# A two-layer hybrid DiT on one core: ada rows loaded two ahead and folded a call later, the gate in four pieces, five attention fetches moved, and the first chunk's columns moved

## The chip, the cores and the metric

The kernel runs on one core of one Trainium2 chip. The metric is the device time of one execution in microseconds (us). A core has TensorE (PE; its weight loads are shown as PEld), VectorE (DVE), ScalarE (ACT), GpSimd (POOL) and SyncE (SP). SP issues most of the loads from DRAM, ScalarE and GpSimd some. Matmuls write to PSUM, which has eight banks of 128 x 512 numbers of 32 bits; the other data are in SBUF.

## The reference

The model has two layers on 256 latent tokens and 256 context tokens, 1024 wide. In short:

```python
for i in range(DEPTH):                       # 2 layers
    mod   = silu_c  @ ada_w[i] + ada_b[i]    # 1024 -> 6 * 1024, for the latent tokens
    mod_c = silu_cc @ ada_w[i] + ada_b[i]    # the same for the context
    sh1, sc1, g1, sh2, sc2, g2 = split(mod)
    h, hc = x * (1 + sc1) + sh1, ctx * (1 + sc1c) + sh1c
    y, yc = retention_mixer(...) if i == 0 else neighbourhood_mixer(...)
    x = layer_norm(ALPHA * x + g1 * y)
    h = x * (1 + sc2) + sh2
    x = layer_norm(ALPHA * x + g2 * (relu(h @ w1[i]) ** 2 @ w2[i]))
    # in layer 0 the same for ctx
```

All matrices are float32. `ada_w` has 2 x 1024 x 6144 numbers, 50 MB, though it is used with two vectors only. The neighbourhood mixer has 32 heads of 32 columns; each latent token attends to a window of latent tokens, with a bias for each place, and to all context tokens.

## The kernel before

**Matmuls in three parts.** TensorE gets each float32 matrix as a high part (`hi`, a rounded copy) and a low part (`lo`, what the rounding left). `mm3` issues three matmuls for each product: high by high, high by low, low by high. A weight unit is 512 KB. `fetch` loads it into a buffer `raw` (SP), ScalarE casts it to `hi`, and VectorE subtracts to get `lo`, which frees `raw`. The pool of `raw` has four buffers, and `hi` and `lo` have five each (`WB`). `take` hands out the next unit and fetches ahead until five are in hand, so a further cast waits until TensorE has used up a unit.

**The ada rows.** `ada_w` is too large for TensorE to be the right place for all of it. `bg_stream` is a generator that works it off in the background, one step for each call of `bg`. A step is one row block of 512 KB (`rawa`, lines 416 to 428 and 482 to 489), in the same four `raw` buffers; VectorE multiplies it by a column of the condition and adds it up (`weigh`, tile `acc`, or `strips` in the early parts), once for each of two vectors. At each step the generator first issues the load of the next row (`nxt`, lines 517 to 522) and then weighs the present one. Eight steps make a part. Then `folded` sums the 32 lanes (`red`) and appends to `due` a function that does the rest: `ada_columns` (four small matmuls per vector into the bank `pada`, and an add into `mods`) or `ada_gate` (a matmul into `pada`, a transpose, an add, and a write of the row to DRAM as `grow`). `bg` calls `flush` first, so what one call appended runs at the start of the next (lines 501 to 503 and 561 to 566). `fold` flushes too. Until the first 31 calls are done the early parts run (`EARLY`); the others run in the MLP of layer 0.

**The MLP of layer 0** (lines 1270 to 1425) has two passes `hf` over the 4096 hidden columns. A pass computes eight pairs of hidden blocks (`p1`, with ReLU and square into `hid`) and then two output halves (`half`); each half has eight units `u` of 24 matmuls into four banks, one for each of four groups of 128 tokens, and one `bg` call after each unit. After a half, `accumulate` multiplies each bank by the gate `G2` on VectorE (`acc<-p,G`) and GpSimd adds the result to `R`. The gate's rows come back from DRAM, spread over the 128 partitions, by `load_gate` at `u == 3` of the first half (line 1359): two loads of 512 KB, issued by ScalarE.

**The attention** of layer 1 (lines 1802 to 1838) is a list of steps by hand. Step n has, in this order: `gather(n + 1)`, `turned(n)`, `early` fetches with their `lo`; `scores(n + 2)` (12 matmuls into four banks `pqk`); `soften(n + 2)` (VectorE adds the bias and takes the least, ScalarE takes the exponential with its sum); `late` fetches with their `lo`; a projection (K, Q or V); `flip(n + 1)` (13 transposes into four banks, copied out as `pt` by ScalarE and VectorE by turns); `invert`; `last` fetches; and `attend(n)`. `STEPS` gives `(early, late, last, projection, after)`.

**The first chunk** (lines 887 to 911). The first layer's modulation is computed in eight chunks of 128 columns, on TensorE. Of chunk 0 the sums are computed (`chunk_sums`), copied (`chunk_row`), the four token groups transposed (`chunk_turn`), and the sums turned into columns (`chunk_columns`, then `mod` on VectorE); with these, `chunk_modulate` writes `hTh`, which the matmuls need. `turn_over` issues matmuls that nothing reads.

**What sets the order.** A scheduler orders the instructions of each engine by the order of the program and by the times at which it expects data and buffers; where an engine's `on` is set, the order of the program is kept. On the chip each engine works in the order it was given. In the first chunks SP, TensorE, ScalarE and VectorE are in program order; in the MLP's loops and the attention steps mostly the scheduler's order holds. A helper records all calls, so most rows of the profile name line 84, and tiles tell them apart.

Of the kernel before, what the change touches and what calls it, by code (L numbers as in the profile page):

```python
# [104 lines left out]
def kernel(  # L105
# [50 lines left out]
    def bank(s="ps"):  # L156
        return psp.tile([P, 512], F32, tag="ps", name=nm(s))
# [279 lines left out]
    def ada_columns(l, w, red, c0, nt):  # L437

        pr = bank("pada")
        for j in range(4):  # L440
            pe.matmul(
                pr[32 * j : 32 * j + 32, 0 : 8 * nt],
                lhsT=cv("fold"),
                rhs=red[:, :nt].rearrange("p t (k j) -> p j (t k)", j=4)[:, j],
                start=True,
                stop=True,
                tile_position=(0, 32 * j),
            )
        dve.tensor_add(
            out=mods[l, w][:, :, c0 : c0 + 4, :],  # L450
            in0=(
                pr[:, 0:16].rearrange("p (t s k) -> p s k t", t=2, s=2)
                if nt == 2
                else pr[:, 0:8].rearrange("p (s k) -> p s k", s=2).unsqueeze(3).broadcast_to([P, 2, 4, 2])
            ),
            in1=acol[:, COLUMNS.index((l, w)), :, c0 : c0 + 4].unsqueeze(3).broadcast_to([P, 2, 4, 2]),
        )
# [24 lines left out]
    def bg_load(l, w, part, offs, n):  # L482

        if (l, w, part) not in EARLY:
            return ada_load(l, n, offs)
        raw = rawp.tile([P, 2, 512], F32, tag="raw", name=nm("rawa"))
        w_ap = ada_w[l][256 * (n % 4) : 256 * (n % 4) + 256, offs[n // 4] : offs[n // 4] + 512]
        sp.dma_start(out=raw[:], in_=w_ap.rearrange("(k p) n -> p k n", p=P))
        return raw
# [8 lines left out]

    due = []

    def flush():
        while due:
            due.pop(0)()

    def bg_stream():


        plan = []
        for l, w, part in (
            list(EARLY)  # L510
            + [(0, 1, 2), (1, 0, 0), (1, 0, 1), (1, 0, 2), (1, 1, 0), (1, 1, 1), (1, 1, 2)]
        ):
            sh, sc, g = 3 * w * D, (3 * w + 1) * D, (3 * w + 2) * D
            offs = (sh + 512 * part, sc + 512 * part) if part < 2 else (g, g + 512)
            for n in range(KC):
                plan.append((l, w, part, offs, n))
        nxt = bg_load(*plan[0])
        yield
        for step, (l, w, part, offs, n) in enumerate(plan):
            raw = nxt  # L520
            if step + 1 < len(plan):
                nxt = bg_load(*plan[step + 1])

            nt = 2 if l == 0 or (w == 0 and part < 2) else 1
            if n == 0:
                red = smp.tile([P, 2, 32], F32, tag="red", name=nm("red"), bufs=2)
            if (l, w, part) in EARLY:
                dve.on = True
                for kk in range(2):
                    for t in range(nt):  # L530
                        weigh(spare(t), raw[:, kk, :], t, 2 * (n % 4) + kk, n % 4 == 0 and kk == 0)
                dve.on = False
                if n % 4 == 3:
                    yield
                    for t in range(nt):
                        folded(red, spare(t), t, 512 * (n // 4), 512)
            else:
                if n == 0:
                    acc = slot(S_VL, [P, 2, D], F32, "acc")
                for t in range(nt):  # L540

                    dve.on = n == 0 and l == 0
                    weigh(acc[:, t], raw[:].rearrange("p a n -> p (a n)"), t, n, n == 0)
                    dve.on = False
                if n == KC - 1:
                    for t in range(nt):
                        folded(red, acc[:, t], t, 0, D)
            if n == KC - 1:
                if part < 2:
                    due.append(lambda a=(l, w, red, 4 * part, nt): ada_columns(*a))  # L550
                else:
                    due.append(lambda a=(l, w, red, nt): ada_gate(*a))
            yield

    bgs = bg_stream()
# [5 lines left out]
    def bg(n=1):  # L561
        for _ in range(n):
            if bg_done[0] < bg_max[0]:
                flush()
                bg_done[0] += 1
                next(bgs, None)

# [273 lines left out]

    KINDS = slice(0, NLAT), slice(NLAT, NT)

    def chunk_turn(k):

        pts[k] = bank("pt")[:, 0:256], prs[k][:, 256:512]
        for t in range(4):
            pe.transpose(pts[k][t // 2][:, tsl(t % 2)], R[t][:, tsl(k)], ident)

    def modulated(e, out_ap, pt, k, a):  # L850
# [47 lines left out]
    turn_over(3)  # L898
    chunk_sums(0, 1)
    chunk_row(0, tsl(1))  # L900
    chunk_turn(0)
    chunk_columns(0)
    turn_over(4)
    w = ws[0]
    w.high(w.Q)
    chunk_modulate(0, lambda: (w.high(w.V), w.low(w.Q)))
# [335 lines left out]


    HS = [S_T0, S_T1, S_SH, S_SL, S_TH, S_TL, S_GS, S_VH]
    LAT, ALL, CTX = slice(0, NLAT), slice(0, NT), slice(NLAT, NT)

    def mm1(us, sl, pb, ks=range(KC), at=0):
# [22 lines left out]
    for hf in range(2):  # L1270
# [67 lines left out]
        for half in range(2):  # L1338
            last = hf == 1 and half == 1
            pb = [bank("p2") for _ in range(4)]  # L1340

            def mm2(t, u, un):
                wh, wl = un
                for kk in range(2):
                    k = 2 * u + kk
                    ht = hid[u]
                    mm3(
                        pb[t][:], (ht[:, kk, 0, tsl(t)], ht[:, kk, 1, tsl(t)]), (wh[:, kk, :], wl[:, kk, :]),
                        k == 0, k == 15,
                    )  # L1350

            nheld = 4 if last else 0
            for u in range(8 - nheld):
                (un,) = take(1)
                for t in range(4):
                    mm2(t, u, un)
                bg()
                if G2 is None and u == 3:
                    G2 = load_gate(0, 1)
            if not last:  # L1360
                for t in range(4):
                    accumulate(pb[t], t, half, G2)
                continue
            bg_until(87)
            held = take(4)
            gb = slot(S_VL, [P, 2, D], F32, "gb")
            ln_tiles(gb, 0, 1)
            xns = []
            for i in range(2):
                xn2 = slot(HS[i], [P, 2, D], F32, "xn")  # L1370
                xns += [xn2[:, 0, :], xn2[:, 1, :]]

            def affine(t, pts):

                return [mod_aff(pts[half], half, t, A, B, halves=t < 2) for half in range(2)]

            def turn(t):
                return [mod_pt(xns[t], half) for half in range(2)]

            def settle(t):  # L1380

                add_to(t, 1, gated(pb[t], t, 1, G2), dve)
                stat(t, 1)
                return moments(t)

            def whiten(t, m):
                shift = shift_of(*m)
                center(t, 0, *m, xns[t], shift)
                center(t, 1, *m, xns[t])

            for t in range(4):
                stat(t, 0)
            ORDER = (pe, act, dve)
            for e in ORDER:
                e.on = True
            for i in range(4):
                mm2(0, 4 + i, held[i])
            A, B = fold(0, 1, 1, 0)
            m = settle(0)
            mm2(1, 4, held[0])  # L1400
            mm2(1, 5, held[1])
            whiten(0, m)
            mm2(1, 6, held[2])
            mm2(1, 7, held[3])
            m = settle(1)
            mm2(2, 4, held[0])
            p = turn(0)
            mm2(2, 5, held[1])
            f = affine(0, p)
            whiten(1, m)  # L1410
            for half in range(2):
                mod_split(f[half], half, 0, pool, True)
            mm2(2, 6, held[2])
            mm2(2, 7, held[3])
            m = settle(2)
            mm2(3, 4, held[0])
            p = turn(1)
            f = affine(1, p)
            for half in range(2):
                mod_split(f[half], half, 1, dve, True)  # L1420
            mm2(3, 5, held[1])
            take(0, 2)
            whiten(2, m)
            mm2(3, 6, held[2])
            mm2(3, 7, held[3])
# [358 lines left out]
    def K(g):  # L1784
        return lambda: k_part(g)

    def Q(p):
        return lambda: q_pair(p)
# [4 lines left out]
    def W(half, t):  # L1793
# [7 lines left out]
    REST = lambda: rest_evac(rest_mm(1))  # L1801
    STEPS = [
        (1, 0, 0, [K(2)], []),
        (2, 0, 0, [K(3)], []),
        (2, 0, 0, [K(4)], []),
        (1, 0, 0, [K(5)], []),
        (2, 0, 0, [Q(2)], []),
        (1, 1, 0, [V(0)], []),
        (0, 0, 0, [V(1)], []),
        (0, 0, 0, [V(2)], [REST]),  # L1810
        (0, 0, 0, [V(3)], []),
# [399 lines left out]
```

## Time and profile before

| | |
|---|---|
| median of 3 runs | 1186.33 us (1186.08 to 1186.82) |
| profiled execution | 1185.37 us, span 1183.3 us |
| granted TensorE clock, mean | 0.997 |
| PE, PEld busy | 1170.2 us, 988.2 us |
| DVE, ACT, POOL busy | 841.4, 480.0, 212.6 us |
| DMA | 195.10 MB, 165 GB/s over the span |

Times in the views are us from the span's start. A timeline's row has start, duration, engine, operation, tiles (what is written, an arrow, what is read), shape and count, and in brackets how long the engine was idle before it and what ended that. A row of the windows has the stretch, its length, the busy time (and the instructions) of PE, PEld, DVE, ACT and POOL, the granted clock as a share of full speed, the DMA engines' busy share and GB/s. A row of the waits has the engine and tile that waited, for whom, the total, how often, and the longest. A row of the chain has start, length and what it was; a DMA's length runs from its issue to its landing. A row of the DMA issues has how many, their size, and the median time from issue to landing. A busy TensorE is not one at its peak, as matmuls overlap, and one that waits inside a matmul is counted as busy.

The MLP of layer 0 runs from about 436 to 796 us, its first output half from about 527 to 570. The attention steps run from about 848 to 970.

### The profile page before, as it was taken

The page shows a single profiled execution, that of the slowest core. Times are in us where ns is not written, and L with a number is a line of the kernel's source. Part 1 is how long each engine was busy: PE and PEld are TensorE (multiplying, and loading weights), DVE is VectorE, ACT ScalarE, POOL GpSimd, SP SyncE. Part 2 cuts the span into 40 slices and gives each one's busy share as a digit, 9 for nine tenths or more (in the row PEclk, how much of TensorE's full clock was granted, in tenths as well). Part 3 has the DMA queues.
Part 4 walks back from the last instruction along what each step waited for, and adds up shares of the span by engine and source line. Part 5 has one row for each costly group of instructions (what it writes and reads, how often), then busy time and mean ns, then how long its engine had stood idle before and what let it go on. Part 6 is the DMA issues. An engine that isn't in the chain of part 4 may idle for free.

```text
span 1183.3 us, 17724 instructions
## 1 busy us (share of the span) xinstructions
PE 1170.2 (99%) x6822; PEld 988.2 (84%) x6822; DVE 841.4 (71%) x1331; ACT 480.0 (41%) x819; POOL 212.6 (18%) x364
## 2 busy tenths in 40 slices
PE   9999999999999999999899999999999999999997
PEld 7788888888888889888788888889878878999886
DVE  3877684876798586897867775668566689877446
ACT  3643332232323255442122333137466666756341
POOL 0102001100200340870203000223344430000001
PEclk9999999999999999999999999999999999999999
DMA  9932551543364226776566665646244334666660
GB/s 277 273 125 92 157 165 48 179 143 107 124 194 146 89 67 222 211 186 227 174 196 202 212 213 189 199 138 203 84 140 125 107 116 160 217 208 200 231 211 37
DMA packets 139091, 195.10 MB, mean 165 GB/s; under 512 B 9936, under 2 KB 81136, under 8 KB 139008
## 3 DMA queue, kind: packets, MB, share of 16 engines
q1 hardware_dynamic: 130880, 182.03, 48.5%
q0 software_dynamic: 6976, 9.39, 3.5%
q10 hardware_dynamic: 1152, 2.56, 0.6%
q8 instruction: 53, 0.87, 0.3%
q14 instruction: 30, 0.25, 0.1%
HBM read 189.12 MB, written 5.75 MB: 165 GB/s over the span
## 4 chain that ended last, share of the span: by engine, by line
PE 85%; DVE 5%; DMA 5%; issue 2%; ACT 2%; POOL 0%; SPq 0%; DVEq 0%; ACTq 0%; POOLq 0%
PE p L84 34%; PE pq L84 8%; PE pv L84 7%; PE pw L84 7%; PE pg L84 7%; PE pn L84 5%; PE pnv L84 4%; PE po L84 3%; DMA rawa<-in_ada_w_dram 2%; DVE acc L84 2%; DMA raw<-in_mlp_w_dram 2%; PE pnw L84 1%; PE pS L84 1%; DVE lo L84 1%; PE ppt L84 1%
## 5 line engine op out<-in xcount | busy, mean ns | idle before, releaser
L84 ACT CAST hi<-raw 128x1024 fp32r<-128x1024 f32 (+2 forms) x228 | 232.1, 1034 | 318.7 <-DMA raw<-in_mlp_w_dram 82.9
L84 DVE TENSOR_TENSOR lo<-raw,hi 128x1024 fp32r<-128x1024 f32 (+2 forms) x228 | 275.0, 1220 | 99.2 <-ACT hi L84 99.1
L84 PE MATMUL p<-hi,hid 128*128 128x512 f32 (+1 forms) x832 | 243.2, 375 | 0.0
L84 PEld LDWEIGHTS p<-hi,hid 128*128 128x128 f32 x832 | 153.0, 189 | 28.2
L84 PE MATMUL p<-hTh,lo 128*128 128x256 f32 (+1 forms) x512 | 165.8, 326 | 0.0
L84 PE MATMUL p<-hTl,hi 128*128 128x256 f32 (+1 forms) x512 | 165.8, 326 | 0.0
L84 PE MATMUL p<-hTh,hi 128*128 128x256 f32 (+1 forms) x512 | 162.9, 328 | 0.0
L84 PE MATMUL p<-lo,hid 128*128 128x512 f32 (+1 forms) x416 | 156.0, 375 | 0.0
L84 DVE SCALAR_TENSOR_TENSOR acc<-rawa,scol,acc 128x1024 f32<-128x1024 f32 x70 | 91.9, 1322 | 66.5 <-DMA rawa<-in_ada_w_dram 66.5
L84 PEld LDWEIGHTS p<-hTh,lo 128*128 128x128 f32 x512 | 96.4, 188 | 8.8
L84 PEld LDWEIGHTS p<-hTl,hi 128*128 128x128 f32 x512 | 96.4, 188 | 8.6
L84 PEld LDWEIGHTS p<-hTh,hi 128*128 128x128 f32 x512 | 94.2, 188 | 8.7
L84 PEld LDWEIGHTS p<-lo,hid 128*128 128x128 f32 x416 | 78.7, 189 | 13.7
L84 ACT CAST hid<-r 128x256 fp32r<-128x256 f32 (+1 forms) x64 | 32.0, 502 | 115.3 <-DVE r L84 115.1
L84 POOL TENSOR_TENSOR rstd<-rstd,misc 128x1 f32<-128x1 f32 x28 | 19.2, 687 | 214.1 <-DVE rstd L84 212.9
L84 DVE SCALAR_TENSOR_TENSOR strips<-rawa,scol,strips 128x512 f32<-128x512 f32 x84 | 57.6, 747 | 0.0
L84 ACT ACTIVATE s<-s,mn 128x512 f32<-128x512 f32 x64 | 45.5, 714 | 26.2 <-DVE mn L84 26.2
L84 POOL TENSOR_SCALAR rstd<-mv 128x1 f32<-128x1 f32 x16 | 3.9, 244 | 290.0 <-DVE mv L84 290.0
L84 POOL TENSOR_TENSOR R<-R,acc 128x512 f32<-128x512 f32 x16 | 24.8, 1566 | 165.9 <-DVE acc L84 165.8
L84 PE MATMUL pw<-hi,oh 128*128 128x512 f32 x128 | 50.9, 398 | 0.0
L84 PE MATMUL pg<-hi,hTh 128*128 128x512 f32 x128 | 50.6, 395 | 0.0
L84 PE MATMUL pw<-hi,ol 128*128 128x512 f32 x128 | 49.9, 390 | 0.0
(236 smaller groups left out, 2328.2 us busy)
## 6 DMA issues: line engine op xcount, KB each, us to landing
raw<-in_mlp_w_dram SPq DMA_DIRECT2D x128, 512.0 KB, 4.5
rawa<-in_ada_w_dram SPq DMA_DIRECT2D x80, 512.0 KB, 3.9
raw<-in_ret_w_in_dram SPq DMA_DIRECT2D x42, 512.0 KB, 3.6
raw<-in_nat_w_in_dram SPq DMA_DIRECT2D x24, 512.0 KB, 4.5
rawq<-in_ada_w_dram SPq DMA_DIRECT2D x16, 512.0 KB, 6.1
raw<-in_ret_w_o_dram SPq DMA_DIRECT2D x16, 512.0 KB, 3.6
bias<-rpb_rows POOLq DMA_DIRECT2D x32, 128.0 KB, 2.9
raw<-in_nat_w_o_dram SPq DMA_DIRECT2D x8, 512.0 KB, 3.7
```

The lines of the kernel that those rows point to most:

```text
L84: r = f(*args, **kwargs)
```

## The change

Four edits are made together.

- `bg_stream` keeps a list of loaded rows. From the first part behind `EARLY` on it loads until two rows beyond the present one are on their way, where it was one.
- Each entry of `due` carries the number of the call that made it. In the MLP `bg` runs only entries that are at least two calls old, so a part is folded into `pada` one call later. In the early parts, and in `fold`, nothing changes.
- The gate of the MLP is loaded in four pieces of 256 KB: at `u == 3` and `u == 4` the first 512 columns of the second and the first row, at `u == 6` and `u == 7` the others.
- In five rows of `STEPS` fetches move: in four of them one or two from `early` to `late`, and a fifth row's one from `early` to the row before as `last`. In chunk 0, two of the four transposes move behind the columns, the pair that did share the bank of the sums gets a bank of its own, and `turn_over` has one matmul fewer.

```diff
-    def flush():
-        while due:
-            due.pop(0)()
+    def flush(before=1 << 30):
+        while due and due[0][0] < before:
+            due.pop(0)[1]()
...
-        nxt = bg_load(*plan[0])
+        loaded = [bg_load(*plan[0])]
         yield
         for step, (l, w, part, offs, n) in enumerate(plan):
-            raw = nxt
-            if step + 1 < len(plan):
-                nxt = bg_load(*plan[step + 1])
+            raw = loaded.pop(0)
+            ahead = 1 if step < len(EARLY) * KC else 2
+            while len(loaded) < min(ahead, len(plan) - 1 - step):
+                loaded.append(bg_load(*plan[step + 1 + len(loaded)]))
...
-                    due.append(lambda a=(l, w, red, 4 * part, nt): ada_columns(*a))
+                    due.append((bg_done[0], lambda a=(l, w, red, 4 * part, nt): ada_columns(*a)))
                 else:
-                    due.append(lambda a=(l, w, red, nt): ada_gate(*a))
+                    due.append((bg_done[0], lambda a=(l, w, red, nt): ada_gate(*a)))
...
             if bg_done[0] < bg_max[0]:
-                flush()
+                flush(bg_done[0] + (bg_max[0] == 31))
...
-    def chunk_turn(k):
-
-        pts[k] = bank("pt")[:, 0:256], prs[k][:, 256:512]
-        for t in range(4):
+    def chunk_turn(k, ts=range(4)):
+
+        if k not in pts:
+            pts[k] = bank("pt")[:, 0:256], (prs[k][:, 256:512] if k else bank("pt")[:, 0:256])
+        for t in ts:
...
-    chunk_turn(0)
+    chunk_turn(0, (0, 1))
     chunk_columns(0)
-    turn_over(4)
+    chunk_turn(0, (2, 3))
+    turn_over(3)
...
-                if G2 is None and u == 3:
-                    G2 = load_gate(0, 1)
+                if hf == 0 and half == 0 and u > 2:
+                    if G2 is None:
+                        G2 = cpool.tile([P, 2, D], F32, tag="G", name=nm("G"))
+                    if u != 5:
+                        t, sl = u % 2 if u < 5 else u - 6, HALF[u > 5]
+                        act.dma_start(out=G2[:, t, sl], in_=grow[0, 1][t : t + 1, sl].broadcast_to([P, 512]))
...
-        (2, 0, 0, [K(3)], []),
-        (2, 0, 0, [K(4)], []),
-        (1, 0, 0, [K(5)], []),
-        (2, 0, 0, [Q(2)], []),
-        (1, 1, 0, [V(0)], []),
+        (0, 2, 0, [K(3)], []),
+        (0, 2, 0, [K(4)], []),
+        (0, 1, 0, [K(5)], []),
+        (0, 2, 1, [Q(2)], []),
+        (0, 1, 0, [V(0)], []),
```

More of the change, by code (lines that the diff above doesn't have):

```diff
@@ L1244 @@
     HS = [S_T0, S_T1, S_SH, S_SL, S_TH, S_TL, S_GS, S_VH]
+    HALF = slice(0, 512), slice(512, 1024)
     LAT, ALL, CTX = slice(0, NLAT), slice(0, NT), slice(NLAT, NT)
```

## The prediction

> **What bounds the kernel now.** I read the page first (busy shares, the chain), then the waits of TensorE alone, then the stretch of the longest of them.
>
> ```profile
> PE 1170.2 (99%) x6822; PEld 988.2 (84%) x6822; DVE 841.4 (71%) x1331; ACT 480.0 (41%) x819; POOL 212.6 (18%) x364
> ```
> ```profile
> PE pada L84 <- DVE acc L84: 3.2, 1, 3.2
> ```
>
> TensorE has work in 99% of the span, so an edit that removes no matmul can win only TensorE's waits. By far the longest that the trace names is `pada`'s, 3.2 us at once, in the MLP. The stretches around it, with the granted clock in the column before the DMA share:
>
> ```profile
> 575.70:578.70 3.00, 0.00 (x0) 0.00 (x0) 2.95 (x4) 1.05 (x1) 0.00 (x0) 1.00 0.14 55
> 578.80:583.20 4.40, 4.38 (x19) 3.47 (x20) 4.40 (x5) 0.00 (x0) 4.35 (x3) 0.61 0.57 165
> 630.00:662.80 32.80, 32.80 (x152) 26.96 (x144) 23.61 (x26) 11.29 (x16) 6.30 (x6) 1.00 0.65 203
> ```
>
> TensorE does nothing for 3 us, and the 4.40 us behind have a granted clock of 0.61 where other stretches have 1.00: another 4.40 x 0.39 = 1.7 us. The place costs 3.2 + 1.7 = 4.9 us.
>
> What makes `pada` late stands in VectorE's timeline and in the chain of waits (a DMA's piece there runs from issue to landing):
>
> ```profile
> 569.91 1.19 DVE L84 TENSOR_TENSOR lo<-raw,hi 128x1024 fp32r<-128x1024 f32 x1
> 571.01 1.41 DVE L84 TENSOR_SCALAR acc<-rawa,scol 128x1024 f32<-128x1024 f32 x2
> 575.75 1.28 DVE L84 SCALAR_TENSOR_TENSOR acc<-rawa,scol,acc 128x1024 f32<-128x1024 f32 x1 [3.33 <-DMA rawa<-in_ada_w_dram]
> 576.95 1.22 DVE L84 TENSOR_TENSOR lo<-raw,hi 128x1024 fp32r<-128x1024 f32 x1
> 578.08 1.28 DVE L84 TENSOR_TENSOR acc<-p,G 128x512 f32<-128x512 f32 x2
> ```
> ```profile
> 540.96 8.89 DMA rawa<-in_ada_w_dram
> ...
> 571.12 4.53 DMA rawa<-in_ada_w_dram
> ```
>
> `pada` does not wait for its own input: `red` was folded before the rows shown. It waits for a PSUM bank. At the start of the second output half all eight banks belong to the two halves, and one comes free with `acc<-p,G`, the gating of the first half. That stands on VectorE behind an ada row issued at 571.12, when VectorE was already beginning the row before it, and landed 4.53 us later. An in-order VectorE waited 3.33 us for it, and TensorE for VectorE.
>
> **The change part by part, the MLP.** Three edits meet here; none adds or takes away a matmul.
>
> Ada rows two ahead: a row is issued one step earlier. The rows and the weights share four raw buffers, and the rows now hold three.
>
> ```profile
> raw<-in_mlp_w_dram SPq DMA_DIRECT2D x15, 512.0 KB, 4.7
> rawa<-in_ada_w_dram SPq DMA_DIRECT2D x13, 512.0 KB, 4.0
> G<-grow ACTq DMA_DIRECT2D x2, 512.0 KB, 7.0
> ```
>
> These are the issues from 520 to 600: 13 rows in 80 us, 6.2 us a row, though TensorE asks for one per weight unit. A unit is 24 matmuls; two units of 24 with the same 512 columns take 5.5 us each by the stretch at 630 (144 weight loads in 32.8 us, 0.228 us each). A row goes: 4.0 us to land, then two `acc` of 1.28 us and a `lo` of 1.22 us between them. Issued a step earlier, the landing lies beside the previous row's 3.8 us of VectorE work; the 3.33 us wait should fall to near nothing, and `acc<-p,G` then ends about 3 us sooner, at some 575.5, just when TensorE comes to `pada`.
>
> Folding one call later: `pada` stands one weight unit later in TensorE's order, so at 575.7 + 5.5 = 581.2. Even with nothing else gained, `acc<-p,G` (first one done by 578.8) is 2.4 us early. Either edit alone takes most of the wait; together they leave about 5 us. I take all of 3.2, and with no idle time before it the slow clock goes too: 4.9 us. Ends: 0, if an equal wait comes up behind it, and 4.9.
>
> [...]
>
> The gate in four pieces: two loads of 512 KB became four of 256 KB at units 3, 4, 6 and 7. ScalarE issues them and waits there for `grow`:
>
> ```profile
> 541.88 1.06 ACT L84 CAST hi<-raw 128x1024 fp32r<-128x1024 f32 x1 [6.13 <-DMA grow<-gate]
> ```
> ```profile
> 566.72 1.06 ACT L84 CAST hi<-raw 128x1024 fp32r<-128x1024 f32 x1 [5.49 <-DMA raw<-in_mlp_w_dram]
> 572.69 1.06 ACT L84 CAST hi<-raw 128x1024 fp32r<-128x1024 f32 x1 [4.91 <-DMA raw<-in_mlp_w_dram]
> 577.21 1.05 ACT L84 CAST hi<-raw 128x1024 fp32r<-128x1024 f32 x1 [3.46 <-DMA raw<-in_mlp_w_dram]
> 586.40 1.06 ACT L84 CAST hi<-raw 128x1024 fp32r<-128x1024 f32 x1 [8.15 <-PE p L84]
> ```
>
> Because the gate's fold also moves a call back, `grow` is complete 5.5 us later, near 547, and a `hi` cast behind the first piece can be held as long. Two more issues lie in idle ScalarE time (6.13 us before this cast). The held cast costs nothing while prepared weights are in hand. How many are: the cast of 586.40 waits for the buffer of the second unit of the second half, five back, so it is the seventh, and the cast of 566.72 the fourth. That unit's `lo`, two casts behind, is the one done by 578.2; TensorE began the half at 575.7 - 5.5 = 570.2 and would come to its fourth unit at 570.2 + 3 x 5.5 = 586.7. The lead is 8.5 us, more than the 5.5. If that cover is gone, 5.5 us come back. The first two pieces are needed when the half ends at 570; 547 plus 7.0 is well ahead. Spread over four units, they also no longer meet the row of 540.96, which took 8.89 us against a median of 4.0. I count 0 for the pieces.
>
> **The attention fetches.** Per step TensorE has one score block, one projection, one flip and one attend. Windows from score block to score block:
>
> ```profile
> 848.20:857.30 9.10, 9.10 (x77) 7.38 (x76) 5.54 (x13) 6.00 (x14) 3.18 (x8) 1.00 0.30 91
> 866.40:875.70 9.30, 9.30 (x83) 7.56 (x76) 6.83 (x17) 5.53 (x14) 4.07 (x10) 1.00 0.51 156
> 875.70:886.00 10.30, 9.98 (x80) 7.73 (x76) 6.75 (x17) 6.46 (x17) 4.50 (x12) 1.00 0.42 120
> 886.00:895.70 9.70, 9.70 (x104) 8.85 (x101) 6.97 (x18) 5.92 (x15) 4.12 (x11) 1.00 0.49 150
> 895.70:905.50 9.80, 9.80 (x80) 7.92 (x76) 6.40 (x18) 6.40 (x16) 4.43 (x11) 1.00 0.42 125
> 905.50:915.30 9.80, 9.80 (x84) 7.73 (x76) 6.93 (x19) 5.91 (x16) 4.30 (x11) 1.00 0.36 107
> 924.90:934.00 9.10, 9.10 (x80) 7.37 (x76) 5.61 (x21) 5.89 (x17) 3.38 (x9) 1.00 0.19 46
> ```
>
> The first and the last row are undisturbed steps (a K and a V projection): 9.1 us. The five between exceed it by 0.2, 1.2, 0.6, 0.7 and 0.7 us: 3.4 us, the most that this edit can win. (The page calls TensorE busy there too: a matmul that waits is counted.) How it comes about, from ScalarE's, VectorE's and TensorE's timelines of the second of these rows:
>
> ```profile
> 872.73 0.73 ACT L84 ACTIVATE s<-s,mn 128x512 f32<-128x512 f32 x1 [2.08 <-DVE mn L84]
> ...
> 876.03 0.85 ACT L84 COPY pt<-ppt 128x384 f32<-128x384 f32 x2
> ```
> ```profile
> 868.61 0.29 DVE L84 TENSOR_TENSOR oTl<-rt,oTh 128x128 fp32r<-128x128 f32 x1 [0.37 <-ACT oTh L84]
> 869.72 2.36 DVE L84 TENSOR_TENSOR lo<-raw,hi 128x1024 fp32r<-128x1024 f32 x2 [0.82 <-ACT hi L84]
> 872.00 0.68 DVE L84 CUSTOM_DVE_ANT_1 s<-pqk,bias 128x512 f32<-128x512 f32 x1
> ```
> ```profile
> 876.56 1.31 PE L84 MATMUL pqk<-kT,qT 32*128 32x512 f32 x10 [0.32 <-ACT pt L84]
> ```
>
> Casts and `lo` go first, so the softening starts at 872.00 though VectorE was free at 868.90; ScalarE then idles 2.08 us, its `pt` copies slip to 876.03, and the next score block lacks their banks. Behind the softening, VectorE begins at 868.9, 3.1 us sooner. ScalarE can start its exponentials at 868.90 + 0.7 = 869.6, and of its 2.08 us of idle time about 1.0 stays (its two casts of 1.05 us begin at 872.73 - 2.08 - 2.1, at 868.6 it is free): `pt` comes about 1.1 us earlier, as much as the longest excess. What is late next: the casts, which fall into 872.5 to 874.5, their `lo` until about 875.9. They are for the following step, whose projection starts when these score matmuls end, at 877.9, and wants its first `lo` half a microsecond later: 2 us of margin. VectorE's own two copies behind those `lo` gain little, so I don't take all 3.4: two thirds, 2.3 us. Ends: 3.4, and a loss of 9 us if in four steps a cast and a `lo` (1.0 + 1.2 us) stand on TensorE's path.
>
> The fifth, the last V unit, goes from the head of its step to the tail of the step before; the same work on ScalarE and VectorE, a little earlier: nothing beyond the above. SP's loads follow the buffers that `lo` frees, some 3 us later, with 9 us to the next use: nothing.
>
> **The first chunk.** Its column matmuls go ahead of two transposes (which get a bank of their own), and one of four fillers goes.
>
> ```profile
> 9.05 0.41 PE L84 MATMUL pada<-cst,R 128*128 128x128 f32 x2
> 9.30 0.51 PE L84 MATMUL pada<-cst,row 128*128 128x2 f32 x4
> ```
> ```profile
> 15.60 0.83 ACT L84 CAST hi<-raw 128x768 fp32r<-128x768 f32 x1 [4.02 <-DMA raw<-in_ret_w_in_dram]
> 16.48 0.56 ACT L84 ACTIVATE hTh<-pt,mod 128x256 fp32r<-128x256 f32 x1
> ```
> ```profile
> 17.17 0.69 PE L84 MATMUL pq<-hTh,hi 128*128 128x512 f32 x2
> ```
>
> The columns (9.30) can start where the third transpose does now (9.05), and what hangs on them, up to the first real matmul, comes 0.25 us earlier. But the second chunk's cast waits for its weights from DRAM, `hTh` follows at 16.48 + 0.56 = 17.04, and TensorE takes it at 17.17. What is won at 10 us is given back at 17: at most 0.1, I take 0.05. Ends: 0 and 0.25.
>
> **Sum.** 4.9 + 2.3 + 0.05 = 7.2 us. The profiled execution took 1185.37 us (span 1183.3), 0.96 under the median of the three runs; from 1186.33 the sum gives 1179.1 us.
>
> **The rivals.**
>
> (a) Only the MLP part works, 1186.3 - 4.9 = 1181.4: the attention's excess is set by VectorE's two copies, which stay behind the `lo`. For it: these copies hardly move. Against: the wait the trace names there is for ScalarE's `pt`.
>
> (b) The stall moves. The second half's matmuls, or a later fold, wait 3.2 us for a VectorE that is as late as now: 1186.3 - 2.3 = 1184.0; if the attention gives nothing either, 1186.3. For it: until 579 the chain runs through ada rows and VectorE without a break, so the MLP's preparation is slower than TensorE. Against: VectorE's own work per unit is 2 x 1.28 + 1.22 = 3.8 us of 5.5.
>
> (c) Slower: weights starve. With three of four raw buffers on ada rows, weight loads go one at a time: 4.7 to land, 1.06 cast, 1.22 `lo`, 7.0 us a unit against 5.5. It decides once the lead of prepared weights (8.5 us, above) is spent, 8.5 / 1.5, so six units in; over the ten left of the sixteen in this stage that is 15 us: 1186.3 + 15 = 1201. Against: a row that has been weighed gives its buffer to the weights, and rows that land early are weighed early.
>
> (d) Slower: attention casts on the path, 4 x 2.2 = 9 us lost against the MLP's 4.9 won: 1190.5.
>
> **How the numbers follow.** The forecast 0.50, (a) 0.14, (b) 0.16, (c) 0.13, (d) 0.07. 0.2% is 2.4 us, about what a measurement of this kernel tells from none. The forecast and (a) lie beyond it: faster 0.64. (b) lies within: same 0.16. (c) and (d): slower 0.20. The likeliest case's own range is 1177.8 (4.9, 3.4 and 0.25) to 1181.4. The range that leaves out only the slower cases runs from 1177.0, with 0.8 us for the measurement, to 1188.0, a little over (b)'s 1186.3.
>
> **What would show it.** TensorE's waits without a `pada` row over 1 us, and no stretch near 580 with a granted clock of 0.61. VectorE's waits for `rawa` in the MLP well under today's 3.33. In the attention, softening that begins right behind `oTl`, casts behind the exponentials, and five windows of about 9.1 to 9.4. The first chunk's columns near 9.05, the second chunk's `pq` still at 17.1. It would be wrong with ScalarE casts waiting on `raw` and TensorE's `p` on `lo` in the MLP (c), or `pn` or `pnv` waiting on `lo` (d), or a new `pada` wait on VectorE (b).

## The result and the profile after

The changed kernel takes 1191.24 us (median of 20 runs, 1186.60 to 1195.03), the kernel before 1187.06 (median of 20 runs, 1182.89 to 1189.28). The ratio is 1.0037, 95% interval 1.0025 to 1.0048: some 4 us slower, outside the predicted range of 1177.0 to 1188.0. The profiled execution has a span of 1189.1 us against 1183.3.

The page of the changed kernel (busy engines, then the chain that ended last) and its waits of TensorE:

```profile
PE 1170.9 (98%) x6821; PEld 985.7 (83%) x6821; DVE 840.9 (71%) x1331; ACT 479.1 (40%) x819; POOL 212.2 (18%) x364
PE 68%; DMA 15%; DVE 9%; issue 4%; ACT 3%; POOL 1%; DVEq 0%; SPq 0%; ACTq 0%; POOLq 0%
```
```profile
PE p L84 <- DVE lo L84: 5.6, 5, 2.8
PE pada L84 <- DVE acc L84: 1.7, 1, 1.7
```

TensorE's busy time is nearly as before (0.7 us more in a span 5.8 us longer); what differs is its waits. In the chain that ended last, DMA has 15% where it had 5%. The `pada` wait shrank from 3.2 to 1.7 us, and a wait of a new kind, for the low parts of weights, took its place with 5.6 us in all. In the timelines of TensorE and VectorE the largest of these stands in the second pass, at 633 us:

```profile
632.96 0.79 PE L84 MATMUL p<-hTh,lo 128*128 128x512 f32 x1 [2.75 <-DVE lo L84]
```
```profile
630.49 1.28 DVE L84 SCALAR_TENSOR_TENSOR acc<-rawa,scol,acc 128x1024 f32<-128x1024 f32 x1 [1.24 <-DMA rawa<-in_ada_w_dram]
631.69 1.22 DVE L84 TENSOR_TENSOR lo<-raw,hi 128x1024 fp32r<-128x1024 f32 x1
```

TensorE waits for the `lo` that ends at 632.9; ahead of it on VectorE stands an ada row that came late. The stretches around this wait and around `pada` (stretch, length, busy PE, PEld, DVE, ACT, POOL, granted clock, DMA share, GB/s):

```profile
582.60:588.00 5.40, 5.39 (x31) 4.48 (x32) 5.40 (x5) 0.00 (x0) 5.36 (x4) 1.00 0.63 193
630.00:632.90 2.90, 0.21 (x1) 0.00 (x0) 2.41 (x3) 0.00 (x0) 0.00 (x0) 0.94 0.63 182
632.90:637.00 4.10, 4.04 (x12) 3.27 (x13) 4.10 (x6) 0.00 (x0) 3.41 (x3) 0.63 0.78 254
```

So the slow clock is back too, only 54 us later. Behind `pada` there is none now; behind 633 it is 0.63 on average over 4.1 us.

Why `pada` still waits is to be seen in the groups of VectorE's instructions (busy us, mean ns, then idle time before them and its releaser) from 440 us to the first gating of the second half, before (to 578.08) and after (to 581.87):

```profile
L84 DVE SCALAR_TENSOR_TENSOR acc<-rawa,scol,acc 128x1024 f32<-128x1024 f32 x29 | 36.6, 1280 | 13.2 <-DMA rawa<-in_ada_w_dram 13.2
L84 DVE TENSOR_TENSOR lo<-raw,hi 128x1024 fp32r<-128x1024 f32 x26 | 31.6, 1218 | 4.0 <-ACT hi L84 4.0
L84 DVE TENSOR_SCALAR acc<-rawa,scol 128x1024 f32<-128x1024 f32 x6 | 4.2, 748 | 0.0
```
```profile
L84 DVE SCALAR_TENSOR_TENSOR acc<-rawa,scol,acc 128x1024 f32<-128x1024 f32 x31 | 39.0, 1278 | 7.7 <-DMA rawa<-in_ada_w_dram 7.7
L84 DVE TENSOR_TENSOR lo<-raw,hi 128x1024 fp32r<-128x1024 f32 x26 | 31.7, 1219 | 9.3 <-ACT hi L84 9.2
L84 DVE TENSOR_SCALAR acc<-rawa,scol 128x1024 f32<-128x1024 f32 x6 | 4.2, 747 | 0.0
```

The wait for rows did fall, by 5.5 us. But as many `lo` as before (26) now wait 5.2 us longer for their cast (`hi`), and two more `acc` (31 against 29: one more row) stand ahead of the gating, 2.4 us. The gating begins 3.8 us later, at 581.87 instead of 578.08. VectorE's timeline there, after:

```profile
571.07 1.41 DVE L84 TENSOR_SCALAR acc<-rawa,scol 128x1024 f32<-128x1024 f32 x2
...
575.03 2.48 DVE L84 SCALAR_TENSOR_TENSOR acc<-rawa,scol,acc 128x1024 f32<-128x1024 f32 x2 [1.42 <-DMA rawa<-in_ada_w_dram]
579.53 1.28 DVE L84 SCALAR_TENSOR_TENSOR acc<-rawa,scol,acc 128x1024 f32<-128x1024 f32 x1 [2.02 <-DMA rawa<-in_ada_w_dram]
...
581.87 1.28 DVE L84 TENSOR_TENSOR acc<-p,G 128x512 f32<-128x512 f32 x2
```

The row at 575.03 is the additional one: before, a single `acc` stood between the first row of the part and the gating, with one wait of 3.33 us.

A number that no single row gives made the rest readable: the **lead** of a weight unit, from the end of its `lo` on VectorE to the start of the first matmul that reads it. In the MLP no matmul record is missing up to there, so the units can be counted off. In us, one profiled execution each (a unit of the hidden blocks is named by its block `fp` and a or b; the experiments follow below):

| unit | before | after | e1 | e4 | e5 | e6 | e9 | e10 |
|---|---|---|---|---|---|---|---|---|
| first pass, half 0, u 0 | 15.2 | 10.8 | 15.7 | 14.8 | 15.7 | 14.7 | 11.1 | 14.3 |
| first pass, half 0, u 7 | 11.3 | 7.7 | 16.5 | 12.0 | 15.5 | 13.8 | 8.4 | 11.3 |
| second pass, fp 1 b | 6.8 | 0.1 | 5.2 | 4.2 | 4.3 | 4.6 | 5.9 | 4.4 |
| second pass, fp 2 b | 3.9 | 0.1 | 0.7 | 1.2 | 0.1 | 3.1 | 4.5 | 3.0 |
| second pass, fp 4 b | 3.5 | 0.1 | 0.5 | 0.4 | 0.1 | 4.0 | 4.3 | 4.1 |
| second pass, fp 7 b | 3.1 | 0.1 | 0.1 | 0.1 | 0.1 | 5.0 | 5.3 | 4.6 |

At 0.1 TensorE is waiting. Before, the lead sinks from 15 to 3 us through the MLP; after, it starts 4 us lower and is used up at the second block of the second pass. From there on the preparation of weights, not TensorE, sets the pace.

### The profile page after: what moved, and what is told of

Its sections match the earlier page's. It is cut to its first block, busy times and chain, and to the rows that moved or that the text cites. A ratio compares the mean times of both kernels' runs of the same rounds, so it can differ in the third digit from the quotient of the medians.

```text
span 1189.1 us, 17718 instructions
## 1 busy us (share of the span) xinstructions
PE 1170.9 (98%) x6821; PEld 985.7 (83%) x6821; DVE 840.9 (71%) x1331; ACT 479.1 (40%) x819; POOL 212.2 (18%) x364
## 4 chain that ended last, share of the span: by engine, by line
PE 68%; DMA 15%; DVE 9%; issue 4%; ACT 3%; POOL 1%; DVEq 0%; SPq 0%; ACTq 0%; POOLq 0%
PE p L84 19%; DMA rawa<-in_ada_w_dram 9%; PE pw L84 7%; PE pq L84 7%; PE pg L84 7%; PE pv L84 7%; DVE acc L84 4%; PE pnv L84 4%; PE pn L84 3%; DMA raw<-in_mlp_w_dram 3%; DVE lo L84 3%; PE po L84 3%; ACT s L84 1%; PE pnw L84 1%; ACT hi L84 1%
```

## The experiments

Theory B: two rows ahead hold raw buffers that the weights lack. Theory F: the late fold spoils VectorE's order. Out of the first results came theory S: in the second pass the supply of prepared weights sets the end, so a wait taken from TensorE ahead of it is not won.

**One row ahead again (e1)**, all other edits kept:

```diff
-            ahead = 1 if step < len(EARLY) * KC else 2
+            ahead = 1
```

> The changed kernel with the ada rows loaded one ahead again; late fold, gate pieces, attention rows and first chunk stay. Theory B (buffers): the two rows ahead keep raw buffers from the weights, and that is what makes lo late in the second pass. Then TensorE's extra time in 600 to 795 us falls from 11.7 us to about the 1.7 us of before, the pada stall stays small because of the late fold, and the time is about 1191 - 10 = 1181 us. Rival F (late fold): the fold one call later puts VectorE's accumulates and lo in a worse order; then the second pass still loses 5 us or more and the time stays at 1186 to 1191 us.

Measured: 1185.34 us, ratio to before 0.9984 (0.9971 to 0.9996). So the other edits together win 2 us, and two rows ahead cost some 6 (1.0037 against 0.9984), as B says. But the time is neither B's 1181 nor clearly F's: `pada` does not wait at all any more, and yet the lead still runs out (fp 7 b at 0.1). Behind that its trace has one more wait that the kernel before has not, 1.6 us at 755 us, in the MLP's last output half, for `mod`. F is tested by itself in e5.

**Two rows ahead alone on the kernel before (e2):**

```diff
-                nxt = bg_load(*plan[step + 1])
+            ahead = 1 if step < len(EARLY) * KC else 2
+            while len(loaded) < min(ahead, len(plan) - 1 - step):
+                loaded.append(bg_load(*plan[step + 1 + len(loaded)]))
```

> The kernel before with two rows ahead and nothing else. Theory B: the second pass loses about 10 us and the pada stall near 579 shrinks by 0 to 4 us, so 1193 to 1197 us against 1187. Rival F: rows ahead alone harm nothing, and the pada stall shrinks: 1183 to 1187 us.

Measured: 1190.96 us, 1.0039 (1.0021 to 1.0056), 4.6 us slower. That is outside both ranges (1193 to 1197 and 1183 to 1187). The waits are not where B put them either: instead of one `pada` wait there are two, 3.3 us for `acc` and 2.7 us for `red`, and only 0.3 us for `lo`. The wait for `acc`, of which the prediction had either edit alone take away most, is as long as before.

**Two rows ahead in the first pass only (e3):**

```diff
-            ahead = 1 if step < len(EARLY) * KC else 2
+            ahead = 2 if len(EARLY) * KC <= step < 48 else 1
```

> The changed kernel with two rows ahead only in the first pass of the MLP (32 weight units at the most one row each), and one ahead in the second pass, where the hidden blocks take five rows per four weight units. Theory B, if the loss arises in the second pass itself: 1180 to 1182 us, no more than e1. If the weights already fall behind in the first pass and the second only shows it: 1184 to 1191 us, with TensorE's lo waits still in the second pass.

Measured: 1191.49 us, 1.0030 (1.0014 to 1.0047): as slow as with two ahead throughout. The harm is done in the first pass, where the lead falls (2.8 us at its last unit, 10.3 before), and paid in the second, where TensorE waits 3.3 us for `hi` and 2.9 us for `lo`.

**The attention rows alone (e4):**

```diff
-        (2, 0, 0, [K(3)], []),
+        (0, 2, 0, [K(3)], []),
...
-        (2, 0, 0, [Q(2)], []),
-        (1, 1, 0, [V(0)], []),
+        (0, 2, 1, [Q(2)], []),
+        (0, 1, 0, [V(0)], []),
```

> The kernel before with the five moved attention rows alone. The steps of the changed profile say that about 3 us are won there: 1184 us. Rival: the gain there is taken back behind the steps (the last steps and the output projection start earlier and wait for their weights): 1187 us.

Measured: 1185.85 us, 0.9983 (0.9968 to 0.9999), about 2 us faster, between the two values expected. Its MLP is that of the kernel before, and still its profile has 4.2 us of waits for `lo` there, where the profile of before has none: the lead of before, 3 us, is within what one execution differs from the next.

**The late fold alone (e5):**

```diff
...
-                flush()
+                flush(bg_done[0] + (bg_max[0] == 31))
...
```

> The kernel before with the late fold alone. Step of the prediction (a wait taken from TensorE is won, 4.9 us): the pada stall near 579 goes and the time is 1182 us. Theory S (supply): in the MLP the end of the second pass is set by how fast weights are prepared, not by TensorE; the stall only lets the lead of prepared weights grow. Then the pada stall goes, the lead in the second pass is 4 to 5 us smaller, lo waits take its place there, and the time is 1185.5 to 1188 us, the same.

Measured: 1186.29 us, 1.0003 (0.9988 to 1.0019). This is the test of the prediction's largest term. From the timeline and the waits of TensorE:

```profile
580.98 0.26 PE L84 MATMUL pada<-red,cst 128*32 128x16 f32 x8
```
```profile
PE p L84 <- DVE lo L84: 3.0, 4, 1.9
```

`pada` stands at 580.98 with no idle time before it and a granted clock of 1.00 from 575 to 590 us: the whole 4.9 us at that place is gone, and none of it is won. TensorE is earlier by that much, the supply is not, and TensorE waits for `lo` instead, for the longest time 106 us later. The trace shows it won and lost: unit fp 2 b of the second pass starts at 638.8 us, 4.9 us ahead of the kernel before (643.7), and unit 1 of the output half behind it at 712.3, 0.3 us ahead (712.6). The late fold does no harm either, so F falls with it.

**Four ada rows moved to the first pass (e6)**, on e1:

```diff
-                bg(2 + fp % 2)
+                bg(2)
...
-                bg()
+                bg(2 if hf == 0 and u in (2, 5) else 1)
```

> e1 with four ada rows moved from the hidden blocks of the second pass (two rows each instead of two and three by turns) to the first pass's output halves (two rows after units 2 and 5 of each half). Theory S: the lead at the end of the second pass's hidden blocks, 0.1 us in e1, stays at 3 us or more, the lo waits there go, and the time falls from e1's 1185.3 to 1181 to 1183 us. Rival (the DMA engines are full over the whole MLP, so rows moved ahead cost as much lead as they save): 1184.5 to 1187 us, and the lead is as small at the same place.

Measured: 1180.49 us, 0.9951 (0.9932 to 0.9971). No wait for `lo` is left and the lead stays at 3 to 5 us. S holds: by the ratios it is 4 us below e1, and the stretch that was short is the one relieved.

**Three raw buffers (e7):**

```diff
-    rawp = ec(tc.tile_pool(name="rawp", bufs=4))
+    rawp = ec(tc.tile_pool(name="rawp", bufs=3))
```

> The kernel before with three raw buffers instead of four: with one row ahead the rows hold two, which leaves the weights one, as two rows ahead of four buffers do. Theory B (the held buffer is the cost): the lead of prepared weights in the first pass's output halves falls as in the changed kernel (from about 15 to 8 us or less, against 13 to 16 before), lo waits fill the second pass, and the time is 1192 us or more. Rival (the cost is that a row goes ahead of a weight once, some 4 us): the lead in the MLP stays within 2 us of before, and what is lost lies in stages without ada rows.

Measured: 1201.43 us, 1.0123 (1.0099 to 1.0146). The lead is 7.9 us at unit 0 of half 0 (15.2 before); then TensorE waits 4.3 us for `red`, and the lead recovers during that wait. In the second pass it runs out again, with 4.3 us of `lo` waits in all, as B expected. A raw buffer is worth 15 us here, but in this kernel other stages lose it too, so it does not price the two rows.

**Two of the four rows in the hidden blocks (e8)**, on e1:

```diff
-                bg(2 if fp > 5 else 1)
+                bg(2 if fp > 3 else 1)
...
+                bg(2 if hf == 0 and half == 1 and u in (2, 5) else 1)
```

> As e6, but of the four rows two go to the first pass's fifth and sixth hidden blocks (counted from nought: fp 4 and 5, where the lead of e1 is 10 to 17 us) and two to its second output half. Theory S: again 1181 to 1183 us, with a lead at the end of the second pass's hidden blocks of 3 us or more. Rival (full DMA engines): the lead drops in the first pass by as much, 1184.5 to 1187 us.

Measured: 1187.26 us, 1.0009 (0.9994 to 1.0024). Half of S held: the lead in the second pass is 7 to 15 us and no `lo` is waited for there. But TensorE now waits in the first pass, 2.6 us for `red` and 3.6 us for the gating; 19.5 rows stand ahead of that gating on VectorE, 17.5 in e1. As the rival had it, the lead of the first pass drops (fp 7 b 0.1, in e1 10.7) and the time is a little above the rival's 1184.5 to 1187. But the DMA engines are no fuller than in e1 (busy share 0.76 from 500 to 527 us, in e1 0.85), and the waits that the trace names are for VectorE.

**Two rows ahead on e6 (e9):**

```diff
-            ahead = 1
+            ahead = 1 if step < len(EARLY) * KC else 2
```

> e6 with two rows ahead. Theory B (rows ahead hold raw buffers and slow the preparation of weights, by 5 to 9 us until the end of the second pass's hidden blocks): e6's lead of 4 to 5 us there is used up, lo waits come back, and the time is 1183 to 1187 us against e6's 1180.5. Rival (two ahead harms only where the rows come 2 and 3 to a pair of hidden blocks): with the rows spread evenly the lead stays as in e6 and the time within 1 us of 1180.5.

Measured: 1188.79 us, 1.0022 (1.0009 to 1.0035), 8.3 us above e6; of TensorE's waits the first, in e6 and in e9:

```profile
PE p L84 <- DVE acc L84: 1.5, 1, 1.5
```
```profile
PE p L84 <- DVE acc L84: 7.1, 1, 7.1
```

The price is above the 1183 to 1187 us that B gave, and the place is not B's: no `lo` is waited for, and in the second pass's hidden blocks the lead stays at 4 to 6 us or more. VectorE behind the last `red`, in e6 and in e9:

```profile
565.73 1.40 DVE L84 TENSOR_SCALAR acc<-rawa,scol 128x1024 f32<-128x1024 f32 x2
567.06 2.47 DVE L84 SCALAR_TENSOR_TENSOR acc<-rawa,scol,acc 128x1024 f32<-128x1024 f32 x2
...
571.92 2.48 DVE L84 SCALAR_TENSOR_TENSOR acc<-rawa,scol,acc 128x1024 f32<-128x1024 f32 x2 [1.26 <-DMA rawa<-in_ada_w_dram]
...
575.45 1.28 DVE L84 TENSOR_TENSOR acc<-p,G 128x512 f32<-128x512 f32 x2
```
```profile
569.11 1.40 DVE L84 TENSOR_SCALAR acc<-rawa,scol 128x1024 f32<-128x1024 f32 x2
570.43 2.47 DVE L84 SCALAR_TENSOR_TENSOR acc<-rawa,scol,acc 128x1024 f32<-128x1024 f32 x2
...
573.96 2.47 DVE L84 SCALAR_TENSOR_TENSOR acc<-rawa,scol,acc 128x1024 f32<-128x1024 f32 x2
577.68 2.48 DVE L84 SCALAR_TENSOR_TENSOR acc<-rawa,scol,acc 128x1024 f32<-128x1024 f32 x2 [1.25 <-DMA rawa<-in_ada_w_dram]
...
581.21 1.88 DVE L84 TENSOR_TENSOR acc<-p,G 128x512 f32<-128x512 f32 x3
```

Between `red` and the gating stand three rows in e6 and four in e9: the scheduler puts a row whose load stands earlier ahead of the gating. `red` itself also comes 3.4 us later in e9 (566.88 instead of 563.50): from 440 us to the gating VectorE's waits for rows fell from 6.6 to 1.7 us, those of `lo` for casts grew from 4.2 to 12.3. Over all: 19.0 rows ahead of the first gating against 20.0, as it was 17.5 against 18.5 before and after the change.

**The best of it on the kernel before (e10):** the attention rows of e4 and the moved rows of e6, nothing else.

```diff
-                bg(2 + fp % 2)
+                bg(2)
...
-                bg()
+                bg(2 if hf == 0 and u in (2, 5) else 1)
...
-        (2, 0, 0, [K(3)], []),
+        (0, 2, 0, [K(3)], []),
...
```

> The kernel before with the five attention rows and the four moved ada rows of e6, and nothing else: fold at the next call, gate in two loads, first chunk as before. With two rows after units 2 and 5 a part ends at unit 5, in the middle of an output half, where banks are free. Theory S: no pada stall even without the late fold, and 1180 to 1182 us, as e6. Rival (the late fold is needed): a pada stall of 2 us or more with the slow clock behind it, and 1183 to 1186 us.

Measured: 1179.24 us, 0.9941 (0.9921 to 0.9962), the lowest median of all, though its interval overlaps e6's. The late fold is not needed: `pada` waits 0.9 us, in mid-half at 565, for `red`, and no slow clock follows (1.00 from 565.1 to 570.0 us).

**The doubled rows earlier (e11)**, on e6:

```diff
-                bg(2 if hf == 0 and u in (2, 5) else 1)
+                bg(2 if hf == 0 and u in ((1, 3), (3, 5))[half] else 1)
```

> e6 with the doubled rows after units 1 and 3 of the first half and 3 and 5 of the second instead of 2 and 5 of each. e6 has one stall left in the MLP, 1.7 us at 576, where TensorE waits for a bank that VectorE's gating of the first half frees. With no doubled row in the last three units of that half VectorE comes to the gating earlier: the stall goes, 1178.5 to 1180.5 us. Rival (the supply is then short elsewhere, or the stall's time is only moved): 1180 to 1183 us.

Measured: 1183.44 us, 0.9974 (0.9958 to 0.9990): a miss. The wait for the gating grew from 1.5 to 3.5 us, with a clock of 0.62 behind it; 19.5 rows stand ahead of it, where e6 has 19.0. With earlier calls the scheduler put more rows ahead of the gating, not fewer.

**VectorE in program order, one and two ahead (e12, e13), and on e10 (e14)**, so that rows and gating can't change places:

```diff
-                    dve.on = n == 0 and l == 0
+                    dve.on = True
...
+                dve.on = True
                 for t in range(4):
                     accumulate(pb[t], t, half, G2)
+                dve.on = False
```

> The kernel before with the weighing of the ada rows and the gating kept in the order of the program on VectorE (16 rows ahead of the first half's gating, 17.5 before). It is the base for e13. The gating comes up to 1.5 rows of 2.56 us sooner, so the pada stall should shrink from 3.2 us to under 1; by the theory of supply this is worth at most 1 to 2 us as long as the second pass is short of weights: 1184 to 1187 us.

> e12 with two rows ahead: VectorE's order of rows, lo and gating is as in e12 around the gating, only the loads differ. Theory O (the cost of two ahead is the row that moves ahead on VectorE): e12's time within 1.5 us. Theory B (held buffers): 4 us or more above e12, with weights that land later.

> e10 with the order of e12 (18 rows ahead of the first half's gating, 19 in e10). e10's only stall over 0.5 us in the MLP is 1.1 us at 565, for red, which stands behind rows in either order. Theory: 1178.5 to 1180 us, as e10. Rival (program order takes from the scheduler what it used to fill VectorE's waits for rows): 1181 us or more.

Measured: e12 1205.45 us, 1.0164 (1.0144 to 1.0184); e13 1248.68 us, 1.0526 (1.0507 to 1.0546); e14 1201.12 us, 1.0119 (1.0099 to 1.0139). Program order costs 19 us on the kernel before and 22 on e10 (17.7 and 15.0 us of `pada` waits for `red`); the times expected of it in e12 and e14 missed. What the pair was for, it shows: with the same order of rows and gating, two ahead cost 43 us. (Not all of it is waiting for weights: TensorE waits 17 us more for `red` and 13 us for `lo` and `hi`, and its mean clock is 0.98 instead of 0.99.) SP's and ScalarE's timelines in e13:

```profile
557.03 0.37 SPq L84 DMA_DIRECT2D raw<-in_mlp_w_dram  x1
563.36 0.37 SPq L84 DMA_DIRECT2D raw<-in_mlp_w_dram  x1
569.59 0.37 SPq L84 DMA_DIRECT2D raw<-in_mlp_w_dram  x1
```
```profile
561.02 1.05 ACT L84 CAST hi<-raw 128x1024 fp32r<-128x1024 f32 x1 [5.28 <-DMA raw<-in_mlp_w_dram]
567.25 1.05 ACT L84 CAST hi<-raw 128x1024 fp32r<-128x1024 f32 x1 [5.18 <-DMA raw<-in_mlp_w_dram]
```

Weights go one at a time, 6.3 us apart, each issued when the `lo` of the one before has freed the buffer, against TensorE's 5.5 us a unit. So the held buffer is a cost of its own. In the changed kernel the scheduler weighs rows earlier, which frees buffers earlier, and has one more row ahead of the gating; that this is how it avoids the worst is argued, not shown. How its 6 us divide between buffers and order was not separated.

## Why the prediction was wrong, point by point

- **"I take all of 3.2, and with no idle time before it the slow clock goes too: 4.9 us."** This step failed. The mechanism was right: with the fold one call later `pada` came at 580.98 (predicted 581.2) and did not wait (e5). The value was wrong: 0 instead of 4.9 us (1.0003), the other end that the step itself named, "if an equal wait comes up behind it". Rival (b), the stall moves, had this outcome for this edit in kind, with a chance of 0.16, though it looked for the wait in the second half or at a later fold. The later wait could be read from the trace of before, in the lead of 3 us in the second pass's last blocks. Taking 4.9 us from TensorE ahead of a lead of 3 brings back 2 us of waiting by these numbers alone. What took the other 3 was not separated. The lead differs by as much between executions: e4 has the same MLP and a lead of 0.1 there, and the trace of before is of an execution of 1185.37 us, against a median of 1187.06. The prediction worked out a lead for one unit of the first pass, 8.5 us, and did not follow it to where it is least.
- **"The landing lies beside the previous row's 3.8 us of VectorE work; the 3.33 us wait should fall to near nothing, and `acc<-p,G` then ends about 3 us sooner."** This step failed with the opposite sign. The wait for rows fell from 13.2 to 7.7 us, but what was late next was not named: the casts (5.2 us more) and one more row ahead of the gating. The gating began 3.8 us later. That "either edit alone takes most of the wait" holds for the late fold (e5) and not for two ahead, which left 3.3 us (e2). Two ahead, costed as a gain, cost 4.6 us alone (e2), 6 us beside the other edits (e1), 8.3 us on e6 (e9). With the 4.6 us of e2, 1187.1 less 2.0 for the attention and 0 for the late fold comes to 1189.7. The 1.5 us up to the measured 1191.2 lie within e2's interval, which runs from 2.5 to 6.6 us.
- **Rival (c), weights starve of raw buffers**, given 0.13, is the side on which it came out, as far as `lo` waits in the MLP and the slower time go. Its rate was too high for the scheduler's order: 7.0 - 5.5 = 1.5 us per unit predicted; the lead fell from 10.8 to 7.7 us in seven units, some 0.4 each, and no faster than in the kernel before (15.2 to 11.3). The 4 us between the two were lost earlier, in the first pass's hidden blocks (fp 5 a: 12.7 before, 8.7 after). So it decided not "six units in" but in the second pass, and at 4 us, not 15. In program order its mechanism stands in the open, at 6.3 us a unit (e13).
- **Gate in four pieces, 0.** Consistent: e1, with the attention, late fold, gate pieces and first chunk together, is at 0.9984, and the attention alone at 0.9983; no run has the pieces alone. But `grow` came at 552.5 us, not near 547, and the pieces were not spread: in the scheduler's order all four stand together, and a cast is held behind them as foreseen (4.46 us against "as long" as 5.5). From ScalarE's timeline of the changed kernel:

```profile
552.54 0.84 ACTq L84 DMA_DIRECT2D G<-grow  x2
553.50 1.05 ACT L84 CAST hi<-raw 128x1024 fp32r<-128x1024 f32 x1 [4.46 <-DMA grow<-gate]
553.51 0.83 ACTq L84 DMA_DIRECT2D G<-grow  x2
```

- **Attention, 2.3 us.** Near: 2.0 us by e4's ratio (0.1 to 3.8). The traces say it more sharply: from the first `pqk` to the first `pnw` matmul it takes 126.1 to 126.5 us in the ten traces with this edit and 127.9 to 128.3 in the six without. The five windows after:

```profile
873.50:882.60 9.10, 9.10 (x80) 7.38 (x76) 6.50 (x17) 6.51 (x15) 3.17 (x8) 1.00 0.56 175
882.60:891.70 9.10, 9.10 (x80) 7.38 (x76) 6.14 (x17) 5.54 (x14) 3.76 (x10) 1.00 0.47 148
891.70:901.80 10.10, 9.94 (x107) 8.86 (x102) 7.50 (x19) 6.84 (x18) 4.57 (x11) 1.00 0.48 130
901.80:911.50 9.70, 9.70 (x80) 7.73 (x76) 7.12 (x18) 6.17 (x15) 3.69 (x10) 1.00 0.62 192
911.50:920.70 9.20, 9.20 (x84) 7.41 (x80) 6.03 (x19) 4.94 (x14) 3.68 (x10) 1.00 0.38 100
```

  Three of the five came down to 9.1 or 9.2 as forecast, two did not (10.1 and 9.7): 48.9 us became 47.2, 1.7 in this execution. So the factor of two thirds came near the sum, but not for its reason: it was to leave a little in each step, and what stayed is in two. What holds these two back is not shown.
- **First chunk, 0.05.** Consistent with it. The columns stand at 8.62 instead of 9.30 us and the second chunk's `pq` at 16.94 instead of 17.17, but that chunk's cast, which waits for DRAM alone, also stands 0.25 us earlier in this execution (15.35 instead of 15.60). No run measured this edit alone.

```profile
8.62 0.61 PE L84 MATMUL pada<-cst,row 128*128 128x2 f32 x4
...
16.94 0.70 PE L84 MATMUL pq<-hTh,hi 128*128 128x512 f32 x2
```

## What to carry to other kernels

A wait of the busiest engine is worth its length only down to the smallest lead behind it (e5: 4.9 us taken ahead of a lead of 3, and 1.0003): follow the lead of prepared data (end of preparation to first use) to the end of the stage before pricing the wait, and look for the gain where that lead is least, as the four moved rows did (0.9984 to 0.9951, 4 us). A load issued earlier can also move its consumer earlier in the order that the scheduler gives an engine (e9: 20.0 rows ahead of the gating against 19.0), and it holds its buffer longer (e13: weights 6.3 us apart): count what then stands behind it, and which other loads lose the buffer. Where one execution differs from the next by as much as the margin in question, take the margin as zero (a lead of 3.1 us before, 0.1 in e4 with the same MLP).

## What was unexpected of the hardware

Idle gaps of TensorE of much the same length were followed by the slow clock in one place and not in another. From the timelines and windows of the kernel before (gap of 3.18 us, with the 0.61 of the prediction behind it), e2 (2.73), e4 (2.98 and 1.94) and e5 (1.95):

```profile
578.82 0.26 PE L84 MATMUL pada<-red,cst 128*32 128x16 f32 x8 [3.18 <-DVE acc L84]
```
```profile
534.50 0.30 PE L84 MATMUL pada<-red,cst 128*32 128x64 f32 x2 [2.73 <-DVE red L84]
```
```profile
534.50:539.00 4.50, 4.50 (x21) 3.66 (x22) 4.10 (x6) 1.71 (x3) 0.00 (x0) 1.00 0.50 133
```
```profile
578.69 0.26 PE L84 MATMUL pada<-red,cst 128*32 128x16 f32 x8 [2.98 <-DVE acc L84]
778.04 0.51 PE L84 MATMUL p<-lo,hid 128*128 128x512 f32 x1 [1.94 <-DVE lo L84]
```
```profile
578.70:583.00 4.30, 4.30 (x26) 3.56 (x27) 4.30 (x5) 0.26 (x1) 4.28 (x3) 1.00 0.50 157
778.00:782.50 4.50, 4.46 (x12) 3.50 (x13) 3.39 (x3) 1.05 (x1) 0.00 (x0) 0.62 0.94 272
```
```profile
687.02 0.50 PE L84 MATMUL p<-hTh,lo 128*128 128x512 f32 x1 [1.95 <-DVE lo L84]
```
```profile
687.00:691.50 4.50, 4.47 (x20) 3.71 (x21) 2.83 (x3) 1.12 (x2) 0.00 (x0) 1.00 0.80 236
```

The changed kernel has 0.63 behind 2.75 us and 1.00 behind 1.70 us. So of these five gaps between 1.9 and 3.0 us two had a slow clock behind them (0.62 and 0.63) and three had not (1.00), and in these rows the shortest gap with a slow clock behind it is 1.94 us, the longest without 2.98. Where the clock was slow it cost 4.50 x 0.38 = 1.7 us in e4 and 4.10 x 0.37 = 1.5 in the changed kernel. In the kernel before the granted clock is 0.50 from 579.34 to 582.76 us, in the changed kernel from 632.55 to 635.96, which is 1.7 us each. But the 1.7 us of clock in the prediction's 4.9 do not come with every such gap: e4's gap at the same place is only 0.2 us shorter and has 1.00 behind it. What decides it was not shown.
